# Activation forms made during the out-projection in its freed buffers, and another chain of weight sums and order of products in the up-projection

## The chip, the cores and the metric

The kernel runs on one NeuronCore of a Trainium2 chip. Its time is the device time of one execution in microseconds (us), over three runs the median. The core has five instruction streams that work side by side and wait for one another through semaphores: PE (TensorE, matmuls; PEld is its loading of weights), DVE (VectorE), ACT (ScalarE), POOL (GpSimd) and SP (which here only issues DMAs). Each stream runs its instructions in the order in which they stand: one that waits holds up everything behind it on its engine.

## The reference, cut to what matters

One layer of a decoder on 512 tokens of width 2048, all in float32. The change touches the last step of the mixer (the out-projection `mixed @ w_out`, added to `x`) and the first of the feed-forward part (`up`, 2048 to 2 x 6144 columns).

```python
def conv_ffn(h, w_up, conv_w, w_down):
    up = h @ w_up
    gate, val = jnp.split(up, 2, axis=-1)
    gate = causal_dwconv(gate, conv_w)
    return (jax.nn.gelu(gate) * val) @ w_down
...
        x = x + mixed @ w_out[l]
        x = x + conv_ffn(rmsnorm(x, norm2_w[l]), ffn_up[l], ffn_conv_w[l], ffn_down[l])
    return rmsnorm(x, final_norm_w)
```

## The kernel before

All data lies transposed: channels on the 128 partitions, the 512 tokens along the row. A float32 product is made of three fp32r matmuls: each operand is split into a high part (a cast on ACT) and a low part (what the cast lost, a subtraction on DVE), and hi\*hi, hi\*lo and lo\*hi are summed in PSUM.

**Out-projection** (`out_phase`). Sixteen units, one for each 128 columns of `w_out`, in the order `DORD`. A unit takes 48 matmuls of 512 columns over the sixteen split activations `ah`, `al`; the last two units run as one interleaved loop. `out_done` then adds the unit to the residual in `acc`, squares it for the RMS norm (square on ACT, sum on POOL) and writes it to memory from POOL's queue.

**Forms.** The up-projection multiplies by Winograd's scheme: the 2048 input channels form two halves, and so do the 512 tokens and the two outputs (gate, value). A 2x2 block product then takes seven products in place of eight, on sums of blocks. The activations enter in seven forms: the blocks a11, a12, a22 and the sums s1 to s4. `pair_forms` makes them from channel tiles p and p + 8 as soon as both are finished: two scalings on ACT (`xs`), four subtractions or additions on DVE (`st`), and for each of the seven forms a cast on ACT (L835) and a subtraction on DVE (L836). Three forms go to buffers of their own, the other four into the buffers `ah`, `al`, which are free only when the last loop of the out-projection has passed them. DVE, ACT and POOL are ordered by a scheduler up to line 870, and by hand from there on; PE and SP always stand as written.

**Up-projection** (`UpProjection`). 48 rounds j, one for each 128 gate columns with their 128 value columns. A round has seven products (b22, b11, t3, t1, t2, b21, t4), each 24 matmuls of 256 columns (L1089). `SLOT` gives each product a place, 7j + offset, so that rounds overlap. The weight block of a product is split three places ahead (`LAG`): cast L1066 on ACT, subtraction L1067 on DVE, into four pairs of buffers. The weights' sums are made by DMA: behind a block's split, POOL issues a DMA (L1070) that adds the next block of the chain to the raw block in place. The chain `rb` runs b22, t3, t2, t4, the chain `ra` b11, t1; b21 stands alone (`rc`). Each round has three PSUM banks, x, y and z (`BANK`); products of one bank add onto each other, and `stage` reads a bank between two products where a partial sum is needed: L1105, L1109, L1111 and L1121 on ACT, L1114 to L1118 and L1124 on DVE. `at(n, ...)` puts the rest (the norm's factor, the convolution with a scaling on ACT at L422 and two operations on DVE at L426, gelu, the product, the store) some places later. In `run`, each place first issues loads, then the split, then what was put off to it, then the product and its stage.

Of the kernel before, what the change touches and what calls it, by code (L numbers as in the profile page):

```python
# [8 lines left out]
F32 = mybir.dt.float32  # L9
# [9 lines left out]
P = 128  # L19
S = 512  # L20
# [39 lines left out]
FORMS = ["a11", "s3", "s1", "s4", "a12", "s2", "a22"]  # L60
EARLY, LATE = FORMS[:3], FORMS[3:]
# [19 lines left out]
class Body:  # L81
# [704 lines left out]
    def out_phase(self):  # L786
        tc, nc, io = self.tc, self.nc, self.io
        with ExitStack() as ctx:
# [13 lines left out]
            acc, acc2 = acc_tiles(lambda d: io["xT"][:, d:d + 2, :], "acc")  # L802
# [3 lines left out]
            self.forms = {f: [None] * HK for f in FORMS}  # L806
            early = {}

            def form_tile(f, p):

                if f in EARLY:
                    if (f, p // 2) not in early:
                        early[f, p // 2] = ep.tile([P, 2, 2, HT], F32R, tag=f"ea{EARLY.index(f) * 4 + p // 2}",
                                                   name=f"fm_{f}_{p // 2}")
                    return early[f, p // 2][:, p % 2]
                n = LATE.index(f)
                return self.ap_.tile([P, 2, HT], F32R, tag=("ah", "al")[n % 2] + str(2 * p + n // 2), name=f"fm_{f}_{p}")

            def pair_forms(p):

                xs = ep.tile([P, 2, S], F32, tag="r3", name=f"xs{p}")
                for i in range(2):
                    nc.scalar.activation(xs[:, i, :], acc[p + 8 * i], AF.Copy, scale=self.prm("n2", p + 8 * i))
                st = ep.tile([P, 4, HT], F32, tag="r1", name=f"st{p}", bufs=2)
                a11, a21, a12, a22 = xs[:, 0, 0:HT], xs[:, 0, HT:S], xs[:, 1, 0:HT], xs[:, 1, HT:S]
                tt = nc.vector.tensor_tensor
                tt(out=st[:, 0, :], in0=a11, in1=a21, op=ALU.subtract)
                tt(out=st[:, 1, :], in0=a21, in1=a22, op=ALU.subtract)
                tt(out=st[:, 2, :], in0=st[:, 1, :], in1=a11, op=ALU.subtract)
                tt(out=st[:, 3, :], in0=st[:, 2, :], in1=a12, op=ALU.add)  # L830
                src = {"a11": a11, "s3": st[:, 0, :], "s1": st[:, 1, :], "s2": st[:, 2, :], "s4": st[:, 3, :],
                       "a12": a12, "a22": a22}
                for f in FORMS:
                    t = form_tile(f, p)
                    nc.scalar.copy(out=t[:, 0, :], in_=src[f])  # L835
                    tt(out=t[:, 1, :], in0=src[f], in1=t[:, 0, :].bitcast(F32), op=ALU.subtract)  # L836
                    self.forms[f][p] = t

            def out_done(d, ps):
                nc.vector.tensor_tensor(out=acc[d], in0=acc[d], in1=ps, op=ALU.add)  # L840
                if d == 0:
                    nc.scalar.activation(ssum, acc[d], AF.Square)
                else:
                    sq = ep.tile([P, S], F32, tag="r1", name=f"sq{d}", bufs=2)
                    nc.scalar.activation(sq, acc[d], AF.Square)
                    nc.gpsimd.tensor_tensor(out=ssum, in0=ssum, in1=sq, op=ALU.add)
                nc.gpsimd.dma_start(out=x1d[:, d, :], in_=acc[d])
                if d >= 8:
                    pair_forms(d - 8)
# [5 lines left out]
            for n in range(2):  # L855
                out_done(DORD[n], self.first_out[n])
            wts = self.out_w
            for n in range(2, KT - 2):
                ps = self.psum(f"ps_o{n}")
                self.gemm([(ps, wts[n])], self.ah, self.al)  # L860
                if n + 2 < KT:
                    wts.append(self.prep_unit(io["w_out"][DORD[n + 2]], f"o{n + 2}"))
                out_done(DORD[n], ps)
# [154 lines left out]
class UpProjection:  # L1018
# [7 lines left out]
    CHAIN = {"b11": ("ra", (0, 0)), "t1": ("ra", (1, 0)), "b22": ("rb", (1, 1)), "t3": ("rb", (1, 0)),  # L1026
             "t2": ("rb", (0, 0)), "t4": ("rb", (0, 1)), "b21": ("rc", (0, 1))}
    NEXT = {"b11": "t1", "b22": "t3", "t3": "t2", "t2": "t4"}
    TAG = {"ra": ("r1", 2), "rb": ("raw", 3), "rc": ("r3", 1)}
    BANK = {"b22": "z", "t1": "z", "b11": "x", "b21": "x", "t3": "y", "t2": "y", "t4": "y"}  # L1030
    LAG, LEAD = 3, 7

    def __init__(self, body, ep, rstd):
        self.b, self.nc, self.ep, self.rstd = body, body.nc, ep, rstd
        self.slots = sorted(((7 * j + o, j, f) for j in range(NFF) for f, o in self.SLOT.items()))
# [36 lines left out]
    def prologue(self):  # L1072
        self.load(self.LEAD)
        self.split(self.LAG)

    def product(self, j, f):
# [8 lines left out]
        for kt in range(HK):  # L1085
            sl = slice(kt * P, kt * P + P)
            t = b.forms[self.ACT_FORM[f]][kt]
            st, en = first and kt == 0, kt == HK - 1
            mm = lambda w, x, s, e: nc.tensor.matmul(ps, w[:, sl], x, start=s, stop=e, skip_group_check=True)  # L1089
            mm(hi, t[:, 0, :], st, False)  # L1090
            mm(hi, t[:, 1, :], False, False)
            mm(lo, t[:, 0, :], False, en)
        b.step(8 * 0.36)

    def stage(self, j, f):
# [6 lines left out]
        if f == "b22":  # L1102
            e = ep.tile([P, 4, HT], F32, tag=f"acc{2 * (j % 2)}", name=f"e{j}")
            self.st[j] = {"z3": e[:, 0, :], "p1": e[:, 1, :], "y7": e[:, 2, :], "u3": e[:, 3, :]}
            nc.scalar.copy(out=e[:, 0, :], in_=ps(z))  # L1105
            return
        s = self.st[j]
        if f == "b11":
            nc.scalar.copy(out=s["p1"], in_=ps(x))  # L1109
        elif f == "t3":  # L1110
            nc.scalar.copy(out=s["y7"], in_=ps(y))  # L1111
        elif f == "t2":
            gv = s["gv"] = ep.tile([P, 2, S], F32, tag=f"acc{4 + 2 * (j % 2)}", name=f"gv{j}")
            tt(out=s["u3"], in0=s["p1"], in1=ps(y), op=ALU.add)  # L1114
            tt(out=s["z3"], in0=s["z3"], in1=s["u3"], op=ALU.add)
            tt(out=s["y7"], in0=s["u3"], in1=s["y7"], op=ALU.subtract)
            tt(out=gv[:, 1, HT:S], in0=ps(z), in1=s["z3"], op=ALU.subtract)
            tt(out=gv[:, 1, 0:HT], in0=ps(z), in1=s["y7"], op=ALU.subtract)  # L1118
            at(1, lambda: tt(out=gv[:, 1, :], in0=gv[:, 1, :], in1=self.rstd, op=ALU.mult))
        elif f == "b21":  # L1120
            nc.scalar.copy(out=s["gv"][:, 0, 0:HT], in_=ps(x))  # L1121
# [91 lines left out]
```

## Time and profile before

| | us |
|---|---|
| time, median of three runs | 2312.85 (2312.81 to 2314.67) |
| time of the profiled execution | 2315.78 |
| its span | 2313.8 |
| PE, DVE, ACT, POOL busy in the span | 2226.8, 1530.0, 955.5, 436.9 |

The span is divided in 40 slices of 57.8 us on the page. By the timeline the out-projection's matmuls end at 741.3 us, the up-projection's run from there to 1726.7 us, and the down-projection follows. The lines that carry the argument stand in the prediction.

### The profile page before, as it was taken

Reading aid. Unit: us, or ns where it says so; the run is one execution under the profiler, and the core shown is the slowest. Engines: PE = TensorE matmul, PEld = TensorE weight load, DVE = VectorE, ACT = ScalarE, POOL = GpSimd, SP = SyncE. Lnnn points to the kernel's source line nnn. Section 1 sums busy time; section 2 is a strip of 40 time slices with the busy share of each in tenths; the row PEclk is TensorE's granted clock in tenths of the full one; section 3 lists DMA queues with packets and bytes.
Section 4 is the critical chain, followed back from the end, with each engine's and each line's share of the span. In section 5 each row is a group of like instructions: output and inputs, shape, how many; then the busy total and the mean of one; then the engine's idle time right before and its main releaser. Section 6 shows DMA issues by size and latency. Waiting matters only on the chain.

```text
span 2313.8 us, 35614 instructions
## 1 busy us (share of the span) xinstructions
PE 2226.8 (96%) x13998; PEld 1998.3 (86%) x13998; DVE 1530.0 (66%) x2416; ACT 955.5 (41%) x1449; POOL 436.9 (19%) x533
## 2 busy tenths in 40 slices
PE   8989999999998599999999999999987999999997
PEld 6878888788887599999999999999985888888886
DVE  7756657665326567777676667767765777777776
ACT  6646455434224454444444444444432222222223
POOL 4370811800102211111111111111110000000004
PEclk9999999999999799999999999999998999999998
DMA  6231232323532588888888898888855433333332
GB/s 192 82 99 64 81 103 80 94 76 110 201 122 68 139 202 199 197 198 199 201 204 202 203 205 203 201 202 200 202 119 194 127 121 116 119 109 119 116 129 83
DMA packets 108184, 340.01 MB, mean 147 GB/s; under 512 B 12720, under 2 KB 19120, under 8 KB 108016
## 3 DMA queue, kind: packets, MB, share of 16 engines
q1 hardware_dynamic: 77552, 229.72, 29.2%
q0 software_dynamic: 30464, 108.02, 26.8%
q8 instruction: 110, 1.80, 0.3%
q14 instruction: 58, 0.48, 0.1%
HBM read 314.36 MB, written 23.33 MB: 146 GB/s over the span
## 4 chain that ended last, share of the span: by engine, by line
PE 84%; DVE 5%; POOL 4%; DMA 2%; issue 2%; ACT 2%; SPq 0%; POOLq 0%; ACTq 0%; DVEq 0%
PE ps_y L1089 17%; PE ps_x L1089 11%; PE ps_z L1089 11%; PE ps_d L202 7%; PE ps_d L204 7%; PE ps_d L203 7%; PE ps_u L202 4%; PE ps_u L203 4%; PE ps_u L204 4%; PE ps_o L203 2%; PE ps_o L202 2%; PE ps_o L204 2%; POOL tm L582 2%; POOL tl L584 2%; PE ps_yt L119 1%
## 5 line engine op out<-in xcount | busy, mean ns | idle before, releaser
L911 DVE TENSOR_TENSOR accd<-accd,ps_d 128x512 f32<-128x512 f32 x368 | 244.8, 686 | 144.1 <-PE ps_d L204 143.1
L202 PE MATMUL ps_d<-gs,hi_d 128*128 128x512 f32 x736 | 293.9, 399 | 22.1 <-ACT hi_d L189 12.8
L204 PE MATMUL ps_d<-gs,lo_d 128*128 128x512 f32 x736 | 293.5, 399 | 0.1
L203 PE MATMUL ps_d<-gs,hi_d 128*128 128x512 f32 x736 | 293.2, 398 | 0.0
L1089 PE MATMUL ps_y<-fm_s,hi_t 128*128 128x256 f32 x1536 | 274.3, 280 | 0.0
L1089 PE MATMUL ps_x<-fm_a,hi_b 128*128 128x256 f32 x1536 | 273.3, 281 | 0.0
L189 ACT CAST hi_d<-raw_d 128x1024 fp32r<-128x1024 f32 x96 | 96.1, 1046 | 415.6 <-PE ps_d L203 400.7
L1070 POOL DMA_DIRECT2D rb<-in_w_up x144 | 126.1, 876 | 706.3 <-DVE lo_t L1067 339.4
L1067 DVE TENSOR_TENSOR lo_t<-rb,hi_t 128x1024 fp32r<-128x1024 f32 x144 | 175.9, 1222 | 123.9 <-ACT hi_t L1066 118.2
L202 PE MATMUL ps_u<-xh,hi_in 128*128 128x512 f32 x608 | 246.2, 405 | 0.0
L204 PE MATMUL ps_u<-xh,lo_in 128*128 128x512 f32 x608 | 238.1, 392 | 0.0
L203 PE MATMUL ps_u<-xl,hi_in 128*128 128x512 f32 x608 | 237.7, 391 | 0.0
L1089 PEld LDWEIGHTS ps_x<-fm_a,hi_b 128*128 128x128 f32 x1536 | 236.9, 191 | 0.1
L1089 PEld LDWEIGHTS ps_y<-fm_s,hi_t 128*128 128x128 f32 x1536 | 236.1, 190 | 0.0
L1089 PE MATMUL ps_x<-fm_a,lo_b 128*128 128x256 f32 x768 | 215.6, 281 | 0.0
L1089 PE MATMUL ps_y<-fm_s,lo_t 128*128 128x256 f32 x768 | 214.8, 280 | 0.0
L202 PEld LDWEIGHTS ps_d<-gs,hi_d 128*128 128x128 f32 x736 | 139.8, 190 | 56.8 <-ACT hi_d L189 13.5
L1066 ACT CAST hi_t<-rb 128x1024 fp32r<-128x1024 f32 x144 | 151.3, 1051 | 70.5 <-PE ps_y L1089 57.7
L1089 PE MATMUL ps_z<-fm_s,hi_b 128*128 128x256 f32 x768 | 142.4, 285 | 32.0 <-ACT fm_s L835 27.3
L204 PEld LDWEIGHTS ps_d<-gs,lo_d 128*128 128x128 f32 x736 | 139.6, 190 | 35.2 <-DVE lo_d L190 1.5
L203 PEld LDWEIGHTS ps_d<-gs,hi_d 128*128 128x128 f32 x736 | 139.8, 190 | 33.6
L190 DVE TENSOR_TENSOR lo_in<-raw_in,hi_in 128x1024 fp32r<-128x1024 f32 x80 | 104.4, 1306 | 79.0 <-ACT hi_in L189 78.4
(350 smaller groups left out, 4838.4 us busy)
## 6 DMA issues: line engine op xcount, KB each, us to landing
rb<-in_w_up POOLq DMA_DIRECT2D x144, 512.0 KB, 7.0
raw_d<-in_w_down SPq DMA_DIRECT2D x96, 512.0 KB, 4.4
raw_in<-in_w_in SPq DMA_DIRECT2D x80, 512.0 KB, 3.7
rb<-in_w_up SPq DMA_DIRECT2D x48, 512.0 KB, 6.2
ra<-in_w_up SPq DMA_DIRECT2D x48, 512.0 KB, 5.6
ra<-in_w_up POOLq DMA_DIRECT2D x48, 512.0 KB, 6.7
rc<-in_w_up SPq DMA_DIRECT2D x48, 512.0 KB, 7.4
raw_o<-in_w_out SPq DMA_DIRECT2D x32, 512.0 KB, 3.8
```

The lines of the kernel that those rows point to most:

```text
L189: nc.scalar.copy(out=hi, in_=raw)
L190: nc.vector.tensor_tensor(out=lo, in0=raw, in1=hi.bitcast(F32), op=ALU.subtract)
L202: nc.tensor.matmul(ps, hi[:, sl], a, start=start, stop=False)
L203: nc.tensor.matmul(ps, hi[:, sl], b, start=False, stop=False)
L204: nc.tensor.matmul(ps, lo[:, sl], a, start=False, stop=stop)
L582: nc.gpsimd.tensor_tensor(out=t, in0=bc(ll[:, j, j + 1:32], j + 1), in1=tl[:, j:j + 1, 0:j + 1].broadcast_to([32, m, j + 1]), op=ALU.mult)
L584: nc.gpsimd.tensor_tensor(out=tl[:, j + 1:32, 0:j + 1], in0=tl[:, j + 1:32, 0:j + 1], in1=t, op=ALU.subtract)
L911: nc.vector.tensor_tensor(out=acc[d], in0=acc[d], in1=ps, op=ALU.add)
L1066: nc.scalar.copy(out=hi, in_=raw)
L1067: nc.vector.tensor_tensor(out=lo, in0=raw, in1=hi.bitcast(F32), op=ALU.subtract)
L1070: nc.gpsimd.dma_start(out=raw, in_=self.block(j, self.NEXT[f]), accum_op=ALU.add)
L1089: mm = lambda w, x, s, e: nc.tensor.matmul(ps, w[:, sl], x, start=s, stop=e, skip_group_check=True)
```

## The change

**Forms.** The residual is held in pairs of tiles p, p + 8 (`xp`). The four sums of a pair are split in one cast and one subtraction of 128x1024 (`split_sums`), for six of the eight pairs during the out-projection into buffers of their own. The blocks a11, a12 and a22 are split straight from the residual, with the norm's weight as a scale (`split_block`), during the last loop of the out-projection: `during(kt)` issues them as soon as the loop has passed the buffers that they take. The halves of the last two units' weights are loaded in another order (both first halves, then both second), so that their buffers are free halfway, and the first two weight blocks of the up-projection are split in the same loop. DVE, ACT and POOL are ordered by hand from before this loop. The squares of the last two units come two places into the up-projection, with their sums on DVE in place of POOL.

**Up-projection.** The order in a round is b11, t1, b22, b21, t2, t3, t4, with b11 of rounds 0 and 1 first. The chain `ra` runs b11, t1, t2, t4 (three buffers), the chain `rb` b22, t3 (two). Bank z now holds t1 and then b22, bank y t2, t3, t4. `stage` copies z after t1, reads y after t2 and after t3, and makes one operation fewer on DVE and one copy fewer on ACT in a round.

```diff
+            def split_sums(p):
+                t = st.pop(p)
+                if p < HK - 2:
+                    fh, fl = (ep.tile([P, 4, HT], F32R, tag=f"ea{2 * p + i}", name=f"fs{i}_{p}") for i in range(2))
+                    nc.scalar.copy(out=fh, in_=t)
+                    tt(out=fl, in0=t, in1=fh.bitcast(F32), op=ALU.subtract)
...
+            def split_block(x, h, l, d):
+                nc.scalar.activation(h, x, AF.Copy, scale=self.prm("n2", d))
+                nc.vector.scalar_tensor_tensor(out=l, in0=x, scalar=self.prm("n2", d), in1=h.bitcast(F32),
+                                               op0=ALU.mult, op1=ALU.subtract)
...
+            def during(kt):
+                if kt == 0:
+                    finished(KT - 3, ps)
+                elif kt == 2:
+                    split_sums(HK - 2)
+                elif kt == 3:
+                    up.load(up.LEAD)
+                p = {4: 0, 5: 1, 7: 2, 8: 3, 10: 4, 11: 5, 13: 6}.get(kt)
+                if p is not None:
+                    first_block(p)
+                    second_blocks(p)
+                if kt in (9, 12):
+                    up.split(1 if kt == 9 else 2)
...
-            self.gemm([(last[i], wts[KT - 2 + i]) for i in range(2)], self.ah, self.al)
-            up = UpProjection(self, ep, rstd)
-            up.prologue()
+            self.gemm([(last[i], wts[KT - 2 + i]) for i in range(2)], self.ah, self.al, before=during)
             for i in range(2):
                 out_done(DORD[KT - 2 + i], last[i])
-            ctx.enter_context(tc.manual_schedule(engines={mybir.EngineType.DVE, mybir.EngineType.Activation,
-                                                          mybir.EngineType.Pool}))
-            self.spawn(norm2())
+            first_block(HK - 1)
+            up.split(3)
+            sums(HK - 1)
+            split_sums(HK - 1)
+            second_blocks(HK - 1)
...
-    SLOT = {"b22": 0, "b11": 2, "t3": 4, "t1": 6, "t2": 8, "b21": 10, "t4": 12}
+    SLOT = {"b11": 0, "t1": 3, "b22": 4, "b21": 5, "t2": 6, "t3": 8, "t4": 9}
...
-    NEXT = {"b11": "t1", "b22": "t3", "t3": "t2", "t2": "t4"}
-    TAG = {"ra": ("r1", 2), "rb": ("raw", 3), "rc": ("r3", 1)}
+    NEXT = {"b11": "t1", "t1": "t2", "t2": "t4", "b22": "t3"}
+    TAG = {"ra": ("raw", 3), "rb": ("r1", 2), "rc": ("r3", 1)}
...
-        if f == "b22":
+        if f == "b11":
...
+        if f == "t1":
+            nc.scalar.copy(out=s["z1"], in_=ps(z))
+        elif f == "b21":
+            s["gv"] = ep.tile([P, 2, S], F32, tag=f"acc{4 + 2 * (j % 2)}", name=f"gv{j}")
+            nc.scalar.copy(out=s["gv"][:, 0, 0:HT], in_=ps(x))
+        elif f == "t2":
+            tt(out=s["v"], in0=s["p1"], in1=ps(y), op=ALU.add)
+            tt(out=s["gv"][:, 1, 0:HT], in0=ps(z), in1=s["v"], op=ALU.subtract)
         elif f == "t3":
+            gv = s["gv"]
             tt(out=s["u3"], in0=s["p1"], in1=ps(y), op=ALU.add)
+            tt(out=gv[:, 1, HT:S], in0=s["z1"], in1=s["u3"], op=ALU.subtract)
             at(1, lambda: tt(out=gv[:, 1, :], in0=gv[:, 1, :], in1=self.rstd, op=ALU.mult))
```

How it moves instructions is shown at three places, in rows of the built programs: line, operation, output <- inputs, and the engines or DMA queues that the instruction waits for (DMAHW are loads from SP's queue, DMASW the adding DMAs from POOL's). In names, `hi_t1_7` is the high part of the weights of product t1 in round 7, and the last number only tells buffers apart.

The first place is PE in round 7, where bank z (`ps_z7`) gets its second product. Before, b22 ends there and a product of another bank (t2 of round 6) follows:

```order
L1089 MATMUL ps_z7_8032<-fm_s4_6_6321,lo_b22_7_7931 128x256
L1089 MATMUL ps_z7_8032<-fm_s4_7_6478,hi_b22_7_7930 128x256 x2
L1089 MATMUL ps_z7_8032<-fm_s4_7_6478,lo_b22_7_7931 128x256
L1089 MATMUL ps_y6_7935<-fm_s2_0_5370,hi_t2_6_7961 128x256 [waits Activation_49]
L1089 MATMUL ps_y6_7935<-fm_s2_0_5370,hi_t2_6_7961 128x256
```

Now t1 ends there, and b22 follows at once onto the same bank; its first matmul waits for ACT. The same is so for t3 and t4 on bank y, where the first matmul of t4 waits for DVE:

```order
L1158 MATMUL ps_z7_8094<-fs0_7_0_6414,hi_t1_7_7991 128x256
L1158 MATMUL ps_z7_8094<-fs1_7_0_6415,hi_t1_7_7991 128x256
L1158 MATMUL ps_z7_8094<-fs0_7_0_6414,lo_t1_7_7992 128x256
L1158 MATMUL ps_z7_8094<-fs0_0_5355,hi_b22_7_8023 128x256 [waits Activation_49]
L1158 MATMUL ps_z7_8094<-fs1_0_5356,hi_b22_7_8023 128x256
```

Between the two products of bank z five others stood before, and three between those of bank y; now there is none between t1 and b22, nor between t3 and t4.

The second place is ACT in the same round. Before, the copy of bank z (L1105) stands behind the gelu of round 5, and behind it come the casts for t3 and t4:

```order
L1066 CAST hi_b11_7_7992<-ra7_7865 128x1024 [waits DMAHW0_49,DVE_49,PE_49]
L422 ACTIVATE h5_7991<-h5_7991,prmt_77 128x512 [waits DVE_49]
L1066 CAST hi_b21_6_8027<-rc6_7899 128x1024 [waits DMAHW2_49,PE_49,Activation_49]
L1132 ACTIVATE h5_7991<-h5_7991 128x512 [waits DVE_49,Activation_49]
L1105 COPY e7_8057<-ps_z7_8032 128x256 [waits PE_49]
L1066 CAST hi_t3_7_8059<-rb7_7794 128x1024 [waits DMASW7_49]
```

Now the copy of z (L1178) stands behind the cast for t2, which waits for an adding DMA, and behind the convolution's scaling (L421), which waits for DVE:

```order
L1139 CAST hi_t1_7_7991<-ra7_7760 128x1024 [waits DMASW0_49,PE_49]
L1174 COPY e7_8021<-ps_x7_7996 128x256 [waits PE_49]
L1139 CAST hi_b22_7_8023<-rb7_7891 128x1024 [waits DMAHW2_49,DVE_49]
L1139 CAST hi_b21_7_8054<-rc7_7923 128x1024 [waits DMAHW3_49,DVE_49,PE_49]
L1139 CAST hi_t2_7_8085<-ra7_7760 128x1024 [waits DMASW1_49,DVE_49,PE_49]
L421 ACTIVATE h6_8084<-h6_8084,prmt_77 128x512 [waits DVE_49]
L1178 COPY e7_8021<-ps_z7_8094 128x256 [waits PE_49]
L1139 CAST hi_b11_8_8122<-ra8_7989 128x1024 [waits DMAHW5_49,Activation_49]
```

The third place is ACT around the end of the out-projection. Before, the scalings and casts of pairs 4 to 7 stand behind its last loop, the last of them these:

```order
L823 ACTIVATE xs7_6464<-acc14_5334,prmt_77 128x512
L835 CAST fm_a11_3_6312<-xs7_6464 128x256 [waits Activation_49]
L835 CAST fm_a12_7_6481<-xs7_6464 128x256 [waits PE_49,Activation_49]
L835 CAST fm_a22_7_6487<-xs7_6464 128x256 [waits PE_49]
L1066 CAST hi_b11_0_6444<-ra0_6433 128x1024 [waits DMAHW0_49]
L1066 CAST hi_t3_0_6449<-rb0_6431 128x1024 [waits DMASW2_49]
L1066 CAST hi_t1_0_6494<-ra0_6433 128x1024 [waits DMASW5_49]
L845 ACTIVATE sq7_6455<-acc6_5326 128x512 [waits DVE_49,Pool_49]
L845 ACTIVATE sq15_6460<-acc14_5334 128x512 [waits Pool_49]
L835 CAST fm_s3_3_6315<-st7_6467 128x256 [waits DVE_49]
```

Now only pair 7 is left behind it, and the first row here is that of the last block made inside the loop:

```order
L850 ACTIVATE fb0_6_6372<-xp6_5332,prmt_77 128x512
L850 ACTIVATE fa_7_6398<-xp7_5334,prmt_77 128x256 [waits DVE_49]
L1139 CAST hi_t1_0_6401<-ra0_6249 128x1024 [waits DMASW2_49,PE_49,Activation_49]
L825 ACTIVATE xs7_6406<-xp7_5334,prmt_77 128x512 [waits DMASW1_49,DMASW0_49,Activation_49]
L825 ACTIVATE xs7_6406<-xp7_5334,prmt_77 128x512 [waits DVE_49]
L844 CAST fs0_7_0_6414<-st7_6409 128x512 [waits DVE_49]
L844 CAST fs0_7_1_6418<-st7_6409 128x512
L850 ACTIVATE fb0_7_6422<-xp7_5334,prmt_77 128x512 [waits PE_49]
L1139 CAST hi_b22_0_6426<-rb0_6253 128x1024 [waits DMAHW1_49]
L1174 COPY e0_6456<-ps_x0_6431 128x256 [waits DMASW5_49,DMASW4_49,PE_49]
```

What stood behind the out-projection's end has moved into it, but for one pair.

More of the change, by code (lines that the diff above doesn't have):

```diff
@@ L819, in pair_forms, with act_tile, sums @@
-            def pair_forms(p):
-                xs = ep.tile([P, 2, S], F32, tag="r3", name=f"xs{p}")
+            self.forms = {f: [None] * HK for f in BLOCKS + SUMS}
+            free = [f"{t}{n}" for n in range(KT) for t in ("ah", "al")]
+            tt = nc.vector.tensor_tensor
+            st = {}
+            def act_tile(name, shape):
+                return self.ap_.tile(shape, F32R, tag=free.pop(0), name=name)
+            def sums(p):
+                big = p == HK - 1
+                xs = ep.tile([P, 2, S], F32, tag="acc12" if big else "r3", name=f"xs{p}")
@@ L827, in pair_forms @@
[L827 to L837, printed above, removed]
+                tt(out=t[:, 1, :], in0=a21, in1=a22, op=ALU.subtract)
@@ L839, in out_done, with second_blocks @@
+            def second_blocks(p):
+                h, l = (act_tile(f"fb{i}_{p}", [P, S]) for i in range(2))
+                split_block(res(p + 8), h, l, p + 8)
+                self.forms["a12"][p] = h[:, 0:HT], l[:, 0:HT]
+                self.forms["a22"][p] = h[:, HT:S], l[:, HT:S]
             def out_done(d, ps):
-                nc.vector.tensor_tensor(out=acc[d], in0=acc[d], in1=ps, op=ALU.add)
+                tt(out=res(d), in0=res(d), in1=ps, op=ALU.add)
+                nc.gpsimd.dma_start(out=x1d[:, d, :], in_=res(d))
@@ L851, in norm2, with finished @@
+            def finished(n, ps):
+                d = DORD[n]
+                out_done(d, ps)
+                squares(d, nc.gpsimd)
+                if d >= HK:
+                    sums(d - HK)
+                    if d - HK < HK - 2:
+                        split_sums(d - HK)
             def norm2():
```

116 lines of the change are left out of this document (64 added, 52 removed).

## The prediction

> **What bounds the kernel now.** First the page's head and its slices: PE is busy 96% of the span, and there are few places where it isn't.
>
> ```profile
> PE 2226.8 (96%) x13998; PEld 1998.3 (86%) x13998; DVE 1530.0 (66%) x2416; ACT 955.5 (41%) x1449; POOL 436.9 (19%) x533
> ...
> PE   8989999999998599999999999999987999999997
> ...
> PEclk9999999999999799999999999999998999999998
> ```
>
> The fourteenth slice (752 to 810 us) is one of two deep dips of PE, and the granted clock (PEclk) falls with it. The stretches around it, then, with matmuls in brackets, the granted clock and the DMA share behind POOL:
>
> ```profile
> 600.00:741.00 141.00, 141.00 (x624) 116.79 (x623) 54.32 (x72) 41.46 (x63) 17.47 (x20) 1.00 0.35 109
> 741.30:800.00 58.70, 26.71 (x176) 24.49 (x175) 34.68 (x71) 28.86 (x56) 17.14 (x16) 0.68 0.47 117
> 800.00:1720.00 920.00, 920.00 (x7857) 920.00 (x7856) 644.09 (x837) 447.59 (x606) 161.83 (x185) 1.00 0.88 198
> ```
>
> In the out-projection (first row) PE never stands still, DVE and ACT are busy 39% and 29%. In the up-projection (third row) it never does either: 7857 matmuls in 920 us are 8.54 in a us, so that a product of 24 takes 2.81 us and a round of seven 19.67. Between them, 176 matmuls take 58.7 us; at 8.54 in a us they would take 20.6. **The passage costs 38.1 us.** What PE waits for there, by the waits and the timeline:
>
> ```profile
> PE ps_z L1089 <- ACT fm_s L835: 27.3, 4, 17.7
> PE ps_z L1089 <- DVE fm_s L836: 4.7, 3, 2.9
> ...
> 741.33 0.40 PE L1089 MATMUL ps_z<-fm_s,hi_b 128*128 128x256 f32 x2
> 778.85 1.04 PE L1089 MATMUL ps_z<-fm_s,hi_b 128*128 128x256 f32 x2 [17.67 <-ACT fm_s L835]
> ```
>
> The first product starts when the out-projection ends and stands until its last form, s4 of pair 7, is cast. So the kernel is bound by PE's own pace, and in this passage by ACT and DVE making forms.
>
> **The change: the forms.** The forms of pairs 0 to 6 move into the out-projection. They need no more of ACT and DVE than before (whole 128x1024 splits for 128x256 ones), and these have over 60% of the stretch free. I cost this at nothing; its cover is PE's unbroken out-projection, and if a unit's weights came late there, each us would be paid. Behind the out-projection's end stay, on ACT, in order: a11 of pair 7, the cast for t1, two scalings, two casts of sums, one of blocks, the cast for b22, a copy, the cast for b21, two squares, a copy, the cast for t2, and the copy of bank z that b22 waits for.
>
> ```profile
> L1066 ACT CAST hi_t<-rb 128x1024 fp32r<-128x1024 f32 x129 | 135.6, 1051 | 60.8 <-PE ps_y L1089 53.6 <-DMA rb<-in_w_up 7.0
> L823 ACT ACTIVATE xs<-acc,prmt 128x512 f32<-128x512 f32 x8 | 5.3, 713 | 0.2 <-DVE fm_a L836 0.2
> L1109 ACT COPY e<-ps_x 128x256 f32<-128x256 f32 x43 | 16.0, 373 | 77.3 <-PE ps_x L1089 77.3
> ```
>
> Four casts at 1.05, seven operations of 512 columns at 0.71 or a little less and four short ones at 0.37 to 0.40 make some 10.3 us; 2 us go to residual and sums on DVE that ACT waits for. b22 can so start 12.3 us behind the out-projection. Three products would end at 8.4: a stall of 3.9. The next comes before t3, whose bank DVE reads only behind three splits that wait for adding DMAs, some 2.8 us by the same kind of count. The gaps may slow the clock:
>
> ```profile
> 297.34 1.11 PE L123 MATMUL tok_v<-cst,vT 128*128 128x128 f32 x4 [3.11 <-ACT vT L495]
> 298.68 0.63 PE L203 MATMUL ps_u<-xl,hi_in 128*128 128x512 f32 x1
> ...
> 300.65 0.40 PE L202 MATMUL ps_u<-xh,hi_in 128*128 128x512 f32 x1
> ```
>
> Behind an idle 3.11 us matmuls take 0.63 in place of 0.40 until 300.65, at half pace for 3.3 us, which loses 1.7. One such makes 3.9 + 2.8 + 1.7 = 8.4 us for the passage in place of 38.1: **29.7 us gained** (bounds 24 to 35). [...]
>
> Queues that steps are moved past: SP's loads for the up-projection come four steps into the last loop and have half of it to land; POOL loses two sums and keeps its writes; DVE gets the two sums behind three splits, in the 3.9. The residual's eight loads keep their size and their place. The operation less on DVE and the copy less on ACT in a round lie on engines that nobody waits for. I cost all these at nothing more. That the first two rounds begin with b11 gives s1 a product's time more, which is in the count above.
>
> **The change: the order of products.** Here two waits are new, in every round. First, t4 follows t3 on bank y and must wait until DVE has read y (L1187). The trace has this wait once, at the up-projection's end, where DVE came late:
>
> ```profile
> 1723.22 0.28 PE L1089 MATMUL ps_x<-fm_a,lo_b 128*128 128x256 f32 x1
> 1723.36 0.41 DVE L1114 TENSOR_TENSOR e<-e,ps_y 128x256 f32<-128x256 f32 x1
> 1723.92 0.48 PE L1089 MATMUL ps_y<-fm_a,hi_t 128*128 128x256 f32 x2 [0.42 <-DVE e L1114]
> ```
>
> From the read's end (1723.77) to PE's start pass 0.15 us, and the first two matmuls take 0.48 in place of 0.40. How soon a read starts, a copy shows:
>
> ```profile
> 1312.69 0.28 PE L1089 MATMUL ps_x<-fm_a,lo_b 128*128 128x256 f32 x1
> ...
> 1313.00 0.37 ACT L1109 COPY e<-ps_x 128x256 f32<-128x256 f32 x1 [1.81 <-PE ps_x L1089]
> ```
>
> 0.31 us behind the start of the product's last matmul. So 0.31 + 0.41 + 0.15 = 0.87, where the next matmul would have come 0.12 behind the last: 0.75 lost, 0.83 with the slow restart. DVE is free in time: the split for b22 ahead of the read ends about 0.2 us before. Behind the waiting matmul stands all of PE.
>
> Second, b22 follows t1 on bank z and waits for ACT's copy of z. Ahead of the copy stand the cast for t2 and the convolution's scaling, which needs DVE's product with the norm, which stands behind the split of t2. This very string is in the trace, for another block:
>
> ```profile
> 1301.58 0.40 PE L1089 MATMUL ps_z<-fm_s,hi_t 128*128 128x256 f32 x2
> ...
> 1301.66 1.05 ACT L1066 CAST hi_b<-ra 128x1024 fp32r<-128x1024 f32 x1 [1.13 <-PE ps_y L1089]
> 1304.61 0.72 ACT L422 ACTIVATE h<-h,prmt 128x512 f32<-128x512 f32 x1 [1.90 <-DVE h L1128]
> 1305.24 1.03 ACT L1066 CAST hi_b<-rc 128x1024 fp32r<-128x1024 f32 x1
> ...
> 1302.74 1.23 DVE L1067 TENSOR_TENSOR lo_b<-ra,hi_b 128x1024 fp32r<-128x1024 f32 x1 [0.54 <-ACT hi_b L1066]
> 1303.89 0.68 DVE L1128 TENSOR_TENSOR h<-gv,rstd 128x512 f32<-128x512 f32 x1
> ```
>
> A cast starts 0.08 us into a product (1301.66 against 1301.58), because its buffer is that of the product just ended; 3.58 us later (1305.24) ACT comes to what stands behind the scaling. In the new order the product is t1 and what stands there is the copy: 0.08 + 3.58 + 0.37 + 0.05 to 0.15 is 4.1 us behind t1's start, where t1 takes 2.81. That is 1.27, with the restart **1.35 us** in each round. If the copy stood free it would cost 0.31 + 0.37 + 0.1 - 0.12 + 0.08 = 0.74; that is the lower bound.
>
> Third, the chain `ra` now adds three times with three places between, not four. From a cast to the next on the same raw block pass the cast, the subtraction, 0.3 us to POOL's issue, and the DMA:
>
> ```profile
> 1304.27 0.87 POOL L1070 DMA_DIRECT2D ra<-in_w_up  x1 [1.30 <-DVE lo_b L1067]
> ...
> rb<-in_w_up POOLq DMA_DIRECT2D x144, 512.0 KB, 7.0
> ra<-in_w_up POOLq DMA_DIRECT2D x48, 512.0 KB, 6.7
> ...
> 769.73 1.04 ACT L1066 CAST hi_t<-ra 128x1024 fp32r<-128x1024 f32 x1 [6.58 <-DMA ra<-in_w_up]
> 764.03 0.93 POOL L1070 DMA_DIRECT2D ra<-in_w_up  x1 [6.33 <-DVE lo_b L1067]
> ```
>
> The issue at 1304.27 is 0.30 behind the split's end at 1303.97, so a cast is 2.6 us plus the landing behind the one before. The split of b11 itself ends 2.4 us into b22 (behind the convolution on DVE); the cast for t1 is due 8.4 us into b22, that for t2 another 9.3 later, with the new stall. So two landings may take 17.7 + 0.1 - 2.7 - 2.7 = 12.3 us together before t2's cast, and with it the copy of z, comes late, us for us. By the medians (6.7 and 7.0) they take 13.7 and cost 1.4 us a round; by the lone one (764.03 to 769.7) 5.7 each and nothing. A round that is longer by 2.2 us lowers the DMA share from 0.88 to about 0.79, and by the new times of issue at most one other adding DMA overlaps each, which is near the lone one. I take nothing, and keep 0 to 1.4.
>
> **Sum.** A round grows by 0.83 + 1.35 = 2.18 us. 48 waits on y are 39.8, 47 on z (round 0's is in the passage) 63.5, and one more read at the end, where t2 and t3 meet on y, 0.8: 104.1 in all. Less 29.7 makes **74.4 us more**: 2390.2 against the profiled execution's 2315.78, which lies 2.9 above the median of the three runs. Against that median: 2387.
>
> **Rivals.**
>
> - *The adding DMAs come late.* By the medians 1.4 us a round on top, 47 x 1.4 = 66: 2453. For it: in the up-projection the share is 0.88 now. Against: longer rounds thin it out. Chance 0.13.
> - *The clock falls with the stalls.* Two gaps of 0.8 and 1.3 us in each 22 us could cost a stretch at half pace in each round: 48 x 1.7 = 82 more, 2469. Against it, a gap of 1.16 us leaves the pace alone, as these rows show:
>
> ```profile
> 438.30 0.66 PE L123 MATMUL tok_v<-cst,vT 128*128 128x128 f32 x4 [1.16 <-ACT vT L495]
> ...
> 439.03 0.40 PE L203 MATMUL ps_u<-xl,hi_in 128*128 128x512 f32 x1
> ```
>
>   [...] Chance 0.05.
> - *The passage is not shortened*, because DVE or ACT block inside the last loop on a buffer or a load: 2313 + 104 = 2417. For it only that both engines run in strict order there. Chance 0.05.
> - *The readers keep ahead of PE.* If PE came to b22 and t4 with the banks already read, the stalls would be restarts only, and the kernel faster: 2313 - 30 + 48 x 0.16 = 2291. The point where it turns is 29.7 / 48 = 0.62 us a round. Both reads need the last matmul of the product before, and one such read and restart alone takes 0.74 to 0.83 by the rows above; only waits that the program doesn't make would allow it. Chance 0.04.
>
> **How the numbers follow.** My forecast has 0.73: 2387. Its own range is from 2355 (z's copy free at 0.74, a passage of 3 us: 2313 - 35 + 36 + 40 = 2354) to about 2420 (0.7 us of late DMA a round). Up to 2440 it takes in the passage that isn't shortened and the milder half of the late DMAs; beyond lie the rest of these, the clock and the fast case, some 0.15 to 0.2. A measurement of this kernel can tell about 0.2% from no change, so faster is 0.05, the same 0.02, slower 0.93.
>
> **What would show it.** In the passage: PE idle about 7 us in place of some 32. In a steady round: a gap of about 0.75 us before t4, released by DVE L1187, and one of about 1.3 before b22, released by ACT L1178; DMA share near 0.79; 21.9 us a round. A gap before b22 well over 1.4, with the cast for t2 released by a DMA, speaks for the late chain; matmuls of 128x256 at twice their pitch for the clock. I am wrong if PE shows no gaps before b22 and t4.

## The result, and the profile after

| | before | after |
|---|---|---|
| time, median (range), us | 2313.22 (2312.81 to 2314.67) | 2392.28 (2390.91 to 2394.93) |
| ratio, 95% interval | | 1.0342 (1.0324 to 1.036) |
| span of the profiled execution | 2313.8 | 2389.0 |
| up-projection's first matmul to its last | 741.33 to 1726.74 | 739.66 to 1802.21 |
| a round (mean start to start, rounds 3 to 44) | 19.68 | 21.93 |

The up-projection grew by 77.1 us; the out-projection ends 1.7 earlier. Everything else keeps its time. The two profiled executions differ by 75.1 us (2315.78 and 2390.91) and the medians by 79.1, since the profiled one lies 2.6 above its median before and 1.4 below it after. The head and two slice rows of the page of after:

```profile
PE 2246.6 (94%) x13998; PEld 2002.6 (84%) x13998; DVE 1528.3 (64%) x2340; ACT 943.1 (39%) x1371; POOL 436.0 (18%) x531
...
PE   9989999999999999999999999999995999999997
...
PEclk9999999999999999999999999999997999999999
```

The deep dip of the fourteenth slice is gone. In its place PE loses a little everywhere behind it, which these digits can't show (9 stands for anything from 90%). The same three stretches as before, as a table by stage (after the stretch's length: busy time of PE, PEld, DVE, ACT and POOL with their instructions in brackets, granted clock, DMA share, GB/s):

```profile
600.00:741.00 141.00, 141.00 (x629) 116.95 (x628) 68.68 (x84) 53.54 (x71) 29.46 (x28) 1.00 0.41 127
741.30:800.00 58.70, 50.09 (x391) 48.93 (x390) 36.65 (x56) 26.54 (x38) 8.86 (x11) 0.94 0.72 158
800.00:1720.00 920.00, 847.38 (x7056) 831.29 (x7054) 583.33 (x714) 394.00 (x503) 146.48 (x168) 1.00 0.80 181
```

In the first row DVE and ACT work 14 and 12 us more than before and PE still never stands: the cover of the moved forms holds. In the second PE makes 391 matmuls in place of 176. In the third it stands 73 us at full clock where it stood never. Who releases it, by the waits of the whole span (total, times, longest):

```profile
PE ps_z L1158 <- ACT e L1178: 53.6, 47, 1.4
PE ps_y L1158 <- DVE e L1187: 29.0, 48, 0.6
```

One gap before b22 and one before t4 in every round, released by the two reads that the prediction named. One round in the timeline, first the gap before b22 on PE, then ACT ahead of it:

```profile
1302.37 0.28 PE L1158 MATMUL ps_z<-fs,lo_t 128*128 128x256 f32 x1
1303.79 0.50 PE L1158 MATMUL ps_z<-fs,hi_b 128*128 128x256 f32 x2 [1.13 <-ACT e L1178]
...
1299.81 1.05 ACT L1139 CAST hi_t<-ra 128x1024 fp32r<-128x1024 f32 x1 [2.65 <-PE ps_y L1158]
1302.75 0.72 ACT L421 ACTIVATE h<-h,prmt 128x512 f32<-128x512 f32 x1 [1.89 <-DVE h L1196]
1303.38 0.35 ACT L1178 COPY e<-ps_z 128x256 f32<-128x256 f32 x1
```

PE's last matmul of t1 starts at 1302.37, and ACT could copy 0.31 us later, as in the row of before. But it waits 1.89 us for DVE, scales the convolution's input first, and copies at 1303.38. And before t4, where DVE comes in time:

```profile
1317.88 0.28 PE L1158 MATMUL ps_y<-fs,lo_t 128*128 128x256 f32 x1
1318.77 0.47 PE L1158 MATMUL ps_y<-fb,hi_t 128*128 128x256 f32 x2 [0.60 <-DVE e L1187]
...
1318.20 0.42 DVE L1187 TENSOR_TENSOR e<-e,ps_y 128x256 f32<-128x256 f32 x1 [0.18 <-PE ps_y L1158]
```

### The profile page after: what moved, and what is told of

It reads as the page before. It is cut to its first block, busy times and chain, and to the rows that moved or that the text cites. A ratio compares the mean times of both kernels' runs of the same rounds, so it can differ in the third digit from the quotient of the medians.

```text
span 2389.0 us, 35554 instructions
## 1 busy us (share of the span) xinstructions
PE 2246.6 (94%) x13998; PEld 2002.6 (84%) x13998; DVE 1528.3 (64%) x2340; ACT 943.1 (39%) x1371; POOL 436.0 (18%) x531
## 4 chain that ended last, share of the span: by engine, by line
PE 76%; DVE 8%; POOL 5%; ACT 4%; issue 4%; DMA 3%; SPq 0%; POOLq 0%; ACTq 0%; DVEq 0%
PE ps_y L1158 17%; PE ps_x L1158 11%; PE ps_d L201 7%; PE ps_d L203 7%; PE ps_d L202 7%; PE ps_z L1158 6%; PE ps_u L201 3%; PE ps_u L202 3%; PE ps_u L203 3%; PE ps_o L201 2%; PE ps_o L203 2%; PE ps_o L202 2%; DVE lo_t L1140 2%; ACT hi_t L1139 2%; POOL tm L581 2%
## 5 line engine op out<-in xcount | busy, mean ns | idle before, releaser
L1158 PE MATMUL ps_y<-fs,hi_t 128*128 128x256 f32 x1536 | 271.3, 279 | 3.1 <-DVE e L1183 3.1
L1143 POOL DMA_DIRECT2D ra<-in_w_up x144 | 125.8, 874 | 779.2 <-DVE lo_t L1140 608.9
L1140 DVE TENSOR_TENSOR lo_t<-ra,hi_t 128x1024 fp32r<-128x1024 f32 x144 | 176.4, 1225 | 107.2 <-ACT hi_t L1139 104.1
L1158 PEld LDWEIGHTS ps_y<-fs,hi_t 128*128 128x128 f32 x1536 | 234.2, 189 | 3.5 <-ACT hi_b L1139 2.7
L1139 ACT CAST hi_t<-ra 128x1024 fp32r<-128x1024 f32 x144 | 151.3, 1051 | 196.3 <-PE ps_y L1158 174.0
L1158 PE MATMUL ps_y<-fs,lo_t 128*128 128x256 f32 x768 | 213.7, 278 | 0.0
L1158 PE MATMUL ps_z<-fs,hi_b 128*128 128x256 f32 x768 | 141.7, 287 | 53.6 <-ACT e L1178 53.6
L1158 PE MATMUL ps_y<-fb,hi_t 128*128 128x256 f32 x768 | 143.3, 287 | 29.0 <-DVE e L1187 29.0
L1158 PEld LDWEIGHTS ps_z<-fs,hi_b 128*128 128x128 f32 x768 | 117.2, 190 | 63.3 <-ACT e L1178 63.3
L1158 PEld LDWEIGHTS ps_y<-fb,hi_t 128*128 128x128 f32 x768 | 118.5, 190 | 37.5 <-issue 37.5
```

The lines of the kernel that those rows point to most:

```text
L1139: nc.scalar.copy(out=hi, in_=raw)
L1140: nc.vector.tensor_tensor(out=lo, in0=raw, in1=hi.bitcast(F32), op=ALU.subtract)
L1143: nc.gpsimd.dma_start(out=raw, in_=self.block(j, self.NEXT[f]), accum_op=ALU.add)
```

## The experiments

"Before" in each is the kernel before on the same chip: its medians were 2314.47, 2314.32, 2313.46 and 2315.45 us in the four groups of runs, 2313.22 beside the changed kernel. Rounds and products are given from start to start by the timeline, as means over rounds 3 to 44.

### The two parts by themselves

Forms alone: the changed out-projection, with the class `UpProjection` of before, which takes the new pairs of tiles and starts with b11:

```diff
+        self.slots = sorted((({(0, "b11"): -2, (1, "b11"): -1}.get((j, f), 7 * j + o), j, f)
...
+            ta, tb = b.forms[self.ACT_FORM[f]][kt]
```

> The forms of the change alone: its out-projection and passage, with the up-projection's chains, order and readers of before (only that b11 of rounds 0 and 1 comes first). Theory: the passage costs some 11 us in place of 38.1 and the rounds keep 19.67 us: 2313.2 - 27 = 2286 (2283 to 2291). Rival (the shortened passage owes its time to the order of products as well, because sums come later there): 2295 to 2313, with PE standing on s4 of pair 7.

Measured: 2285.04 us (2284.87 to 2287.91), ratio 0.9876 (0.986 to 0.9893). Rounds of 19.68 us, and an up-projection shorter by 29.2.

Order alone: forms and passage of before with the changed class:

```diff
-        self.load(self.LEAD)
+        self.load(4)
...
-                tag, bufs = self.TAG[r]
+                tag, bufs = self.TAG[r] if r != "rb" else (("acc12", "acc14")[j % 2], 1)
```

> The order alone: forms and passage of before, with the order, the chains and the readers of the changed up-projection (the chain rb in two buffers of its own, and four loads ahead of the forms in place of seven). Theory: rounds of 21.9 us, a passage of 35 to 38 us: 2313.2 + 47 x 2.26 + 0.8 = 2420 (2412 to 2424), so that the two parts add up to the whole: 27 less and 106 more. Rival (the parts help or hinder each other): under 2405 or over 2430.

Measured: 2417.15 us (2415.88 to 2419.0), ratio 1.0444 (1.0428 to 1.0459). Rounds of 21.98. Its waits are those of the changed kernel, with pair 7's forms besides:

```profile
PE ps_z L1092 <- ACT e L1112: 55.4, 48, 1.4
PE ps_y L1092 <- DVE e L1121: 29.0, 48, 0.6
PE ps_x L1092 <- ACT fm_a L835: 14.8, 4, 5.7
```

The change is a gain of 29.4 us and a loss of 102.7 in one. They sum to 73.3 where the whole measured 79.1; the order alone also begins with b11 of two rounds, and so its passage costs some 8 us less than that of before (its first eight products take 55.6 us in place of 62.7, a wait on y among them).

### The price of the wait on z

The convolution, gelu, product and store one place later, so that ACT issues the copy of z ahead of the scaling:

```diff
-            at(1, conv)
-            at(2, gelu)
-            at(3, mul)
-            at(4, lambda: nc.sync.dma_start(out=self.gd[j], in_=gv[:, 1, :]))
+            at(2, conv)
+            at(3, gelu)
+            at(4, mul)
+            at(5, lambda: nc.sync.dma_start(out=self.gd[j], in_=gv[:, 1, :]))
```

> After the change, with the convolution, the gelu, the product and the store of a round each one place later, so that ACT issues the copy of bank z ahead of the convolution's scaling. Theory (b22 waits for the copy, and the copy stands behind the scaling): the copy starts about 0.3 us behind t1's last matmul; from t1's start to b22's start 3.5 us in place of 4.06; 47 x 0.5 = 24 us less than the changed kernel: about 2366, and the waits for the copy fall from 53.6 to about 30 us. Rival (what holds b22 is the cast for t2 ahead of the copy, because its adding DMA is late, or the cost of adding onto a bank just written): no change, 2390 to 2394.

Measured: 2361.97 us (2359.49 to 2363.96), ratio 1.0204 (1.0189 to 1.022): 30.3 less than the changed kernel, where 24 were expected (from t1's start to b22's pass 3.40 us, not 3.5).

```profile
PE ps_y L1158 <- DVE e L1187: 29.1, 48, 0.6
PE ps_z L1158 <- ACT e L1178: 22.1, 47, 0.8
```

The wait on y hasn't moved, that on z is 0.47 us in place of 1.14: the rest was the scaling ahead of it on ACT.

### One wait taken away: b21 ahead of b22

```diff
-    SLOT = {"b11": 0, "t1": 3, "b22": 4, "b21": 5, "t2": 6, "t3": 8, "t4": 9}
+    SLOT = {"b11": 0, "t1": 3, "b21": 4, "b22": 5, "t2": 6, "t3": 8, "t4": 9}
```

> After the change, with b21 ahead of b22 in each round, so that bank z is read while another bank is added to. Theory: the wait for the copy of z goes (1.25 us a round from start to start) and the wait on y stays: 47 x 1.25 = 59 us less than the changed kernel, about 2333; the passage may take 1 to 2 us more, since b21 of round 0 needs the blocks of pair 7. Rival (the chain of three adding steps is the limit, and the two waits only hide it): the time moves to the casts for t2 or t3, which then wait for an adding DMA: 2345 to 2390.

Measured: 2349.64 us (2345.58 to 2358.28), ratio 1.0157 (1.0134 to 1.0179). 42.6 us less, not 59; the rounds are no longer alike (21.21 on average, in the profiled execution, which is the slowest of the four). The waits of ACT point to the reason:

```profile
ACT hi_t L1139 <- DMA ra<-in_w_up: 369.9, 129, 8.3
```

And the place in its timeline where it costs PE most, POOL's issue first, then ACT, then PE:

```profile
1427.49 0.87 POOL L1143 DMA_DIRECT2D ra<-in_w_up  x1 [7.82 <-DVE lo_t L1140]
...
1436.85 1.04 ACT L1139 CAST hi_t<-ra 128x1024 fp32r<-128x1024 f32 x1 [8.28 <-DMA ra<-in_w_up]
1439.79 0.72 ACT L421 ACTIVATE h<-h,prmt 128x512 f32<-128x512 f32 x1 [1.89 <-DVE h L1196]
1440.42 0.35 ACT L1178 COPY e<-ps_z 128x256 f32<-128x256 f32 x1
...
1440.82 0.79 PE L1158 MATMUL ps_z<-fs,hi_b 128*128 128x256 f32 x2 [3.86 <-ACT e L1178]
```

The adding DMA issued at 1427.49 lands over 9 us later. ACT stands at the cast that needs it, and the copy of z waits behind the cast. PE's wait is put down to the copy; its cause is a transfer some steps back. Such waits on z are rare (4 in all, 4.6 us). Most of PE's waiting is before t4, where the wait on y has grown from 29.0 us in all to 42.4. In the changed kernel ACT waits 22.3 us in all for the landings on ra, with the copy first 113.7, here 369.9: the more of the reader waits is gone, the more of this comes out. The chain of work that ended last, followed back from the program's end, spends 44.9% of the time from 800 to 1720 us in DMAs on ra, and 1.4% in the changed kernel. So the rival holds in part. (The swap also leaves rb three places from b22 to t3 in place of four.)

### Both waits taken away, with links of three and of four places

No two products of a bank next to each other, by two orders (the first needs a third buffer for `gv`; in both, b21 of round 0 comes before b22 of round 0):

```diff
-    SLOT = {"b11": 0, "t1": 3, "b22": 4, "b21": 5, "t2": 6, "t3": 8, "t4": 9}
+    SLOT = {"b11": 0, "b21": 2, "t1": 3, "b22": 5, "t2": 6, "t3": 8, "t4": 11}
...
+    SLOT = {"b11": 0, "t1": 4, "b22": 6, "t2": 8, "b21": 9, "t3": 10, "t4": 12}
```

> After the change, with no two products of one bank next to each other (b11, t3, b21, t1, t4, b22, t2 in time), so that both reader waits have a product's time; the chain ra still has three places from b11 to t1 and from t1 to t2. Theory, from the swap of b21 and b22: with the reader waits gone the rounds shorten until the adding DMAs are late; a landing may take 3 x 2.81 - 2.6 = 5.8 us, and at the DMA share of before they take 6.7 to 7.0; that costs up to 1 us a link: 2295 to 2340, with casts that wait for the DMA on ra. Rival (the swap lost its time to something else, and the landing keeps to 5.5): 2284 to 2292.

> As the run with no two products of a bank next to each other, but with four places between all links of the chain ra (b11, t1, t2, t4) and of rb (b22, t3). Theory (the waits for readers and the lateness of adding DMAs are all that the order costs): rounds of 19.7 us, 2286 (2282 to 2292), as with the forms alone. Rival (the order has a further cost, for example three adding steps on one chain or DVE's reads): 2295 or more.

Measured, three places: 2409.57 us (2407.11 to 2411.78), ratio 1.0413 (1.0397 to 1.0428), slower than the changed kernel and far outside what was expected. Four places: 2282.3 us (2280.88 to 2283.03), ratio 0.9862 (0.9848 to 0.9877), rounds of 19.68. The waits of ACT and PE with three places:

```profile
ACT hi_t L1139 <- DMA ra<-in_w_up: 179.2, 69, 5.8
ACT hi_t L1139 <- DMA rb<-in_w_up: 120.9, 39, 9.2
...
PE ps_y L1158 <- DVE e L1183: 77.0, 47, 4.6
```

Its adding DMAs (times, KB each, median us from issue to landing):

```profile
ra<-in_w_up POOLq DMA_DIRECT2D x144, 512.0 KB, 7.1
rb<-in_w_up POOLq DMA_DIRECT2D x48, 512.0 KB, 9.2
```

The same with four places, where a landing has 4 x 2.81 - 2.6 = 8.6 us in place of 5.8:

```profile
ra<-in_w_up POOLq DMA_DIRECT2D x144, 512.0 KB, 7.7
rb<-in_w_up POOLq DMA_DIRECT2D x48, 512.0 KB, 7.2
```

There the landings on ra are no faster, but ACT waits only 11.8 us in all for them. In the rounds PE stands on a reader twice, 0.6 us each, and nothing else of the new order costs anything. I had put the price of late landings at the deficit of one landing (1 us a link). It was 2.7 us a round. With three places, the chain of work that ended last spends 57.0% of the time from 800 to 1720 us in DMAs on ra, 5.1% in those on rb and 8.3% on PE (77.5% on PE in the changed kernel). Some of its pieces in round 25 (start, us, what):

```profile
1303.26 9.11 DMA ra<-in_w_up
...
1312.45 0.07 ACT hi_t L1139
...
1313.77 0.96 ACT hi_b L1139
...
1316.27 6.67 DMA ra<-in_w_up
```

The first DMA adds t2's block. When it has landed, ACT casts t2, and only behind that the b11 of the next round, whose split lets the DMA for the next t1 start; behind that one come the split of t1 and the DMA for t2 again. So a round holds two landings in a row, 7.2 and 8.0 us at the median, and some 7 us of splits and issues: 22.35 in all. The granted clock, 0.98 in these 920 us, adds to what PE loses (last section). With four places the cast for t2 also stands behind that of the next b11, and the loop is open; whether that or the longer links took the cost away was not separated.

### Which chain: rb with four places, ra with three

```diff
-    SLOT = {"b11": 0, "b21": 2, "t1": 3, "b22": 5, "t2": 6, "t3": 8, "t4": 11}
+    SLOT = {"b11": 0, "b21": 1, "t1": 3, "b22": 5, "t2": 6, "t3": 9, "t4": 11}
```

> As the run with no two products of a bank next to each other and three places in the links of the chains, but with b21 and t3 changed over, so that rb (b22 to t3) has four places; ra keeps three, three and five. Theory (it is ra's links of three places that come late): still 2380 to 2415, with casts that wait for the DMA on ra. Rival (it was rb's link of three places): 2282 to 2295, rounds of 19.7 us.

Measured: 2442.59 us (2436.32 to 2444.73), ratio 1.0539 (1.0521 to 1.0557), neither range. The edit did one thing that I had overlooked: b21 now follows b11 at once, on bank x, so there is a reader wait again (L1174 copies x). The waits of ACT and PE:

```profile
ACT hi_t L1139 <- DMA ra<-in_w_up: 295.2, 92, 5.9
ACT hi_t L1139 <- DMA rb<-in_w_up: 9.5, 2, 5.6
...
PE ps_x L1158 <- ACT e L1174: 99.2, 46, 5.0
```

And one such wait in the timeline, ACT and then PE:

```profile
1316.04 1.04 ACT L1139 CAST hi_t<-ra 128x1024 fp32r<-128x1024 f32 x1 [2.87 <-DMA ra<-in_w_up]
1316.99 0.37 ACT L1174 COPY e<-ps_x 128x256 f32<-128x256 f32 x1
...
1317.40 0.50 PE L1158 MATMUL ps_x<-fb,hi_b 128*128 128x256 f32 x2 [1.73 <-ACT e L1174]
```

Still it decides against rb: its lateness is gone (9.5 us), and a reader wait alone, if one on x costs what those on y and z do (0.74 to 1.42 us a round, next part), would have left 2282 + 35 to 67, 2317 to 2349. The chain of work that ended last agrees: from 800 to 1720 us it spends 60.3% in DMAs on ra and nothing in those on rb. So the rest is ra's, whose late cast stands ahead of the copy of x, together with the granted clock, 0.95 in these 920 us (0.98 with three places in each link of both chains). How much a late ra costs without the wait on x was not tried.

### The wait on y alone

The order with four places in each link, but t4 next to t3 on bank y:

```diff
-    SLOT = {"b11": 0, "t1": 4, "b22": 6, "t2": 8, "b21": 9, "t3": 10, "t4": 12}
+    SLOT = {"b11": 0, "t1": 4, "b22": 8, "t2": 9, "b21": 10, "t3": 12, "t4": 13}
```

> As the run with four places in each link of the chains, but in another order (b11, b22, t2, b21, t1, t3, t4 in time), in which t4 follows t3 on bank y at once and nothing else is adjacent. Theory (the wait on y alone, 0.72 before t4 and 0.13 behind it in each round): 2282.3 + 48 x 0.85 = 2323 (2318 to 2328), and the rounds keep one length, 20.5 us; then the 16 us that the swap of b21 and b22 didn't gain were those of its three-place chain. Rival (the swap lost them to something that goes with a lone wait on y, such as a disturbed restart): 2335 to 2350.

Measured: 2320.37 us (2318.22 to 2323.14), ratio 1.003 (1.0017 to 1.0042).

```profile
PE ps_y L1158 <- DVE e L1188: 29.0, 48, 0.6
```

That is PE's one regular wait, and the rounds keep 20.52 us. The order has the wait that the swap of b21 and b22 also has, and its run is 29.3 us faster. Most of that lies in the rounds (20.52 against 21.21 in the swap's slowest execution) and goes with the three-place links; some lies in the passage, where the first eight products take 29.4 us in place of 36.6.

The orders that leave one wait price both. Beside the products of the order with no wait:

| start to start, us | t1 + b22 | t3 + t4 | round |
|---|---|---|---|
| no wait (four places) | 2.76 + 2.77 | 2.77 + 2.87 | 19.68 |
| wait on y alone | 2.77 + 2.77 | 3.52 + 2.95 | 20.52 |
| changed kernel, copy of z first | 3.40 + 2.87 | 3.53 + 2.95 | 21.26 |
| changed kernel | 4.07 + 2.88 | 3.53 + 2.94 | 21.93 |

A wait on y costs 0.83 us, one on z 1.42, and 0.74 with its copy first.

### The passage: the norm's sum later

In two of these kernels the four matmuls of the norm's sum (eight rows in the trace) were put one product later in PE's queue:

```diff
-                yield 5.0
+                yield 8.0
```

> The forms alone, with the four matmuls of the norm's sum one product later in PE's queue. In the forms alone PE stood 6.8 us for the sum of squares. Theory: 4 to 7 us less than the forms alone, about 2279. Rival (the next product stands for its weights or forms just as long): 2283 to 2285.

> The run before, with the four matmuls of the norm's sum one product later in PE's queue. Theory (in the passage PE stands for the sum of squares, 2.6 us, where products could run): 2 to 5 us less than that run, about 2282. Rival (the passage is bound by the casts of pair 7, which ACT makes in the same time whatever PE does): within 1 us of it.

Measured: with the forms alone 2280.89 us (2280.55 to 2283.29), ratio 0.9856 (0.984 to 0.9873), 4.15 less. With the order of four places 2283.85 us (2283.01 to 2285.48), ratio 0.9871 (0.9856 to 0.9885), 1.55 more: no gain. In the first, PE had stood 6.8 us for DVE's sum (forms alone):

```profile
PE ps_n L167 <- DVE ssum L875: 6.8, 1, 6.8
```

With the sum moved it stands for weights in place of it, but less:

```profile
PE ps_y L1160 <- ACT hi_t L1137: 2.5, 1, 2.5
PE ps_y L1160 <- DVE lo_t L1138: 0.8, 1, 0.8
```

In the second, the 2.6 us at the sum came back at the norm's broadcast and at the reads behind it on DVE:

```profile
PE n_ps L118 <- DVE rt_n L135: 2.4, 1, 2.4
...
PE ps_y L1158 <- DVE e L1184: 1.5, 1, 1.5
```

Both kernels with the forms and rounds of 19.68 us, and both with the sum moved, beat the one before, by 1.2 to 1.4%.

## Why the prediction was right, by its steps

**The forms cost nothing where they went.** Right: PE stands nowhere in the out-projection, and the forms alone gained 29.4 us.

**The passage, 38.1 to 8.4, gain 29.7.** The gain was right, and both ends were some 2 us short, so that the error fell out of the difference by luck. From the first product's start to the ninth's pass 62.65 us before and 34.0 after; eight products take 22.5. The ninth product starts at 803.98 before (the first at 741.33) and at 773.66 after (739.66):

```profile
803.98 0.40 PE L1089 MATMUL ps_y<-fm_s,hi_t 128*128 128x256 f32 x2
...
773.66 0.40 PE L1158 MATMUL ps_z<-fs,hi_t 128*128 128x256 f32 x2
```

That is 40.2 before, and 11.5 after, of which 0.7 is the regular wait on y: 10.8, a gain of 29.4. The 176 matmuls that I counted before had 16 small ones of the norm among them, which I had taken for products. After, these cost some 2 us again. Of the named parts, the stall before b22 was shorter and the clock fell twice; that the two cancel is luck as well:

| | forecast | measured |
|---|---|---|
| stall before b22_0 | 3.9 | 2.6, before the norm's sum |
| stall before t3_0 | 2.8 | 2.5 |
| half clock | 1.7 | 3.4 |

The first two come from the timeline of after:

```profile
750.96 1.05 PE L167 MATMUL ps_n<-cst,ssum 128*128 128x1 f32 x8 [2.62 <-DVE ssum L875]
765.50 0.47 PE L1158 MATMUL ps_y<-fs,hi_t 128*128 128x256 f32 x2 [2.51 <-DVE e L1183]
```

The last comes from two stretches behind these gaps, in the table by stage (the clock is the third number from the end). The forecast has one such stretch. There were two, one behind the gap of 2.62 us and one behind that of 2.51, both at 0.50:

```profile
752.79:756.21 3.42, 3.42 (x19) 3.42 (x18) 1.33 (x9) 0.00 (x0) 0.41 (x1) 0.50 1.05 274
766.45:769.86 3.41, 3.41 (x18) 3.41 (x17) 0.49 (x1) 0.00 (x0) 0.86 (x1) 0.50 0.85 144
```

I hadn't seen that the norm's sum stands ahead of b22 in PE's queue. It cost little, since the copy of z that b22 needs ended only at 750.77.

**The wait on y, 0.83 a round.** Measured 0.83, 39.8 us in all.

**The wait on z, 1.35 a round, 0.74 with a free copy.** Measured 1.42 and 0.74. The string of cast, DVE's product, scaling and copy stood as read from another block's casts before; its 0.07 too little makes 47 x 0.07 = 3.3 us.

**Late adding DMAs, none.** Right for the changed kernel, where the landing took 5.5 us and the DMA share is 0.80 (forecast 0.79), and the rival that they'd cost 66 us fell. The first reason that I gave, a lower DMA share, is not borne out, though: with three places the share was lower still, 0.76, and the landings took 7.1 and 9.2 us. The second, that few adding DMAs overlap, was not tried. So that nothing had to be added is in part luck. And the runs show how near it was. From an adding DMA's issue on ra to the cast that needs it the changed kernel has 5.9 us (t1), 6.7 (t2) and 7.6 (t4), medians of rounds 3 to 43. The first two make 12.6 where I had 12.3 (my own terms sum to 12.4), and two landings take 11.1: 1.5 us a round to spare. Without the reader waits three products leave 5.8 for each. The two waits are what gave the chain its time.

**The sum.** 48 x 0.83 + 47 x 1.42 + 0.8 = 107.4, less 29.4: 78.0 against 77.1 of the up-projection and 79.1 of the medians; forecast 74.4. The time of 2392.28 lies in the range, 5 us over the forecast, and most of the difference is the size of the wait on z.

**The other rivals.** The clock kept to 1.00 through 48 rounds with two gaps each: no fall. The passage was shortened. The readers didn't keep ahead where two products of a bank stood next to each other (47 waits on z, 48 on y); one product between them was enough in the order with four places (rounds of 19.68 us).

## What to carry to other kernels

- Where a partial sum is read out between two products on one bank, put a product of another bank between them. Without one PE paid the whole way from its last matmul over the read to its restart, 0.74 to 0.83 us here, and on top what the reading engine had ahead of the read in its queue (0.68 here).
- A chain of transfers has a time per link (here 5.8 us for a landing with three places, 8.6 with four). An order that gives it fewer places can hide behind other waits. Take these away and it appears (2.7 us a round here), and it then holds every reader that stands behind the late step on its engine. Where the next round's first step stands behind the late one too, every landing of the chain up to there counts in the round's length (here 7.2 and 8.0 us of 22.35). Change the places and the waits together.
- A stretch that counts matmuls counts every matmul: sort out the small ones of other steps before the pace is taken from it.

## What the runs showed of the hardware

How long an adding DMA of 512 KB takes doesn't follow from the DMA share: 5.5 us at 0.80 (changed kernel), 7.1 (ra) and 9.2 (rb) at 0.76 with no two products of a bank next to each other and links of three places, 7.7 (ra) at 0.84 (800 to 1690 us) with four. At one place in the timeline of the order with three places, an adding DMA, a store and three loads start within 1.8 us (1303.26 to 1304.99) and the adding one lands 9.1 us later. That such bunches make the landings slow was not tried.

In the changed kernel's passage the gaps of 2.62 and 2.51 us had 3.4 us at a clock of 0.50 behind each of them (shown above). Its two gaps of 0.6 and 1.1 us in each round left the clock at 1.00. By the table by stage, the changed kernel's rounds:

```profile
769.86:1800.00 1030.14, 946.93 (x7879) 928.57 (x7879) 650.94 (x799) 439.91 (x561) 161.49 (x185) 1.00 0.79 177
```

The order with three places has longer gaps, and a clock of 0.98. Its rounds, and then two stretches over which a gap of 2.50 us (from 1165.67) is spread:

```profile
800.00:1720.00 920.00, 844.72 (x6923) 833.48 (x6922) 554.46 (x699) 380.52 (x493) 145.35 (x166) 0.98 0.76 177
...
1163.68:1167.09 3.41, 1.99 (x17) 1.78 (x15) 2.58 (x4) 2.10 (x3) 0.00 (x0) 1.00 0.57 111
1167.09:1170.50 3.41, 2.33 (x20) 2.36 (x21) 3.38 (x6) 2.35 (x4) 0.59 (x1) 1.00 0.00 0
```

The clock is 1.00 in both, and so for 2.3 us behind the gap. The shorter gap of 1.73 us before 1317.40, shown above for the run with rb at four places, has a stretch at half clock behind it, from 1318.77:

```profile
1315.36:1318.77 3.41, 1.68 (x14) 1.48 (x13) 1.66 (x2) 2.26 (x3) 0.14 (x1) 1.00 0.03 10
1318.77:1322.18 3.41, 3.41 (x18) 3.41 (x17) 1.30 (x2) 0.32 (x2) 0.74 (x1) 0.50 0.69 132
```

So the length of a gap alone doesn't settle what the clock does behind it. What else it goes by was not shown.
